# Second blocks: products of the gated unit end with the sixth attention head, gelus and mixing stand sooner, branch additions on GpSimd

## The chip, the cores and the metric

The kernel runs on one core of a Trainium2 chip. The metric is the device time of one execution in microseconds (us), the median of several runs. Engines are called TensorE (PE in the profile), VectorE (DVE), ScalarE (ACT), GpSimd (POOL) and SyncE (SP).

## What is computed

The reference is a small network over 256 tokens of 1024 features: two first blocks (differential attention with a dense gated layer, and a gated linear recurrence with a mixture of eight experts), a norm, and then two "second blocks" of one form. Only the second blocks are touched. Each of them has two halves that read the same normed input:

- a sparse attention with eight heads of 64 in two groups. For every head and each of two chunks of 128 queries there are three branches: a compressed one (32 compressed keys, computed for all heads at once) and two with full scores (masked differently). The three results are weighted by gates (a sigmoid of a projection, 24 columns) and added up:

```
o = gate[0] * o_compressed + gate[1] * o_first + gate[2] * o_second
```

- a gated unit: u and v are projections of 512 columns each; both go through a gelu, v through a layer norm, and then v is mixed over the tokens by a masked 128x128 matrix per group, gets a bias and is multiplied by u:

```
mlp = (mix(layer_norm(gelu(v))) + b) * gelu(u)
```

Each half is normed by its mean square, the two are put side by side (1024 features), multiplied by an output matrix and added to the residual. A gated feed-forward layer follows.

## The kernel before

The function `second` holds one second block. Matrix products of the projections are split into three (hi x hi, hi x lo, lo x hi; L264 to L266), so each weight is split on ScalarE (the hi part, L229) and VectorE (the lo part, L230), and each activation likewise (xh L286, xl L287, after a transpose `tr` L293 of 128x128 tiles).

The heads are taken in sixteen steps: chunk 0 with heads 0 to 3 and 4 to 7, then chunk 1 with the same; I call them the first to the sixteenth head. For each of them there are:

- `score` (L1652 to L1666): products into `sw` (L1657), for each of two branches a mask with row maximum on VectorE (p, L1664) and an exponential with a sum on ScalarE (p, L1665). Chunk 0 has 128 keys a branch, chunk 1 has 256.
- `turn` (L1668 to L1678): transposes into `pt` (L1672), then the copy pT to SBUF, by VectorE for chunk 0 (L1677) and ScalarE for chunk 1 (L1675).
- `value` (L1680 to L1687): products into `po` (L1686), which four heads share.
- `combine` (L1689 to L1699), once for four heads: a small factor from sums and gates, the product `att` (L1696) and two additions of 128x256 into `at` (L1699), one for each branch.

Around the heads four generators are advanced a piece at a time. `gated` (L1553 to L1581) makes the twelve pieces of the products `tw` for three groups of columns (348, 350 and 350 wide); after the second group it puts the two `ln` (gelu of v, statistics, layer norm) on a list called `small`, after the third the gates, two gelus of u, two `mix` (the products `mx` at L1599, then two VectorE operations into `mlp`, L1602 and L1604) and `half_norm` of the mlp. `half_norm` is: the sum of squares on ScalarE (junk, L326), a small t on VectorE (L319), a root r on GpSimd (L320), two scalings on ScalarE (L1540), then transposes and their hi and lo splits. `cmps` makes the compressed branch of both chunks: products `cs` (L1625), a softmax pc (L1629 to L1638), transposes `ct` (L1642), pcT (L1644), products `oc` (L1648) that start `at` (L1650). `ex` finishes what the compressed keys need.

What stands where is set by a table, PLAN: one string for each of the sixteen heads. After the scores of a head its letters are worked off: x is a step of `ex`, z of `gated`, c of `cmps`, s of the list `small`, t turns the oldest scored head if more than three are scored, v takes the value products of the oldest turned head, and o combines the oldest finished four. What is left over is done after the last head. Then comes `half_norm` of the attention half, and the output products `ac` (L258 to L260) run over the mlp half's features first. A scheduler then orders the instructions of each engine; every engine works its own list strictly in that order and waits for what an instruction reads, and for a free buffer.

Of the kernel before, what the change touches and what calls it, by code (L numbers as in the profile page):

```python
# [15 lines left out]
OP = mybir.AluOpType  # L16
# [5 lines left out]
FILL = (4, 0, 0, 0, 0, 1, 1, 1, 1)  # L22
N_AHEAD = (2, 0)
AHEAD = 3
PLAN = ["xzz", "xzz", "xzt", "xztv", "ztv", "ztv", "zsvst", "zcvst", "zcvst", "zcvst", "csvct", "csvst", "osvst", "ovst",
        "svst", "svst"]
TURN = ((0, 0), (1, 1))
N_KV = 2
N_P = 6
# [104 lines left out]
def body(ctx: ExitStack, tc: tile.TileContext, I, out, stop=None):  # L134
    nc = tc.nc
    V, A, T, GP = nc.vector, nc.scalar, nc.tensor, nc.gpsimd
# [18 lines left out]
    def G(s="g", dt=F32):  # L155
        return gp.tile([128, 512], dt, tag="g", name=nm(s))

    def G2(s="t", dt=F32):
        return tp.tile([128, 512], dt, tag="t", name=nm(s))
# [7 lines left out]
    def S(n, s="s"):  # L167
        return sp.tile([128, 16 if n <= 16 else 64], F32, tag="s" if n <= 16 else "sw", name=nm(s), bufs=N_S if n <= 16 else 1)[:, :n]
# [10 lines left out]
    def r3(ap, n):  # L179
        return ap.rearrange("p (a b) -> p a b", a=n)  # L180
# [1158 lines left out]
    def second(i, pj, fill, X):  # L1339
# [121 lines left out]
        for c, ps in enumerate(wide):  # L1461
            g = G("z1")
# [13 lines left out]
        for c, ps in enumerate(tok_wide(X, w, 0, 512, "zq")):  # L1476
            g = G2("zq")
# [3 lines left out]
            for kg in range(2):  # L1481
                t = G2("qhl", F32R)
# [9 lines left out]
        for c in range(2):  # L1492
            A.activation(seg2[:, c * 256:c * 256 + 256], ps[:, c * 256:c * 256 + 256], AF.Copy, scale=r[:, c:c + 1])
            srcs = [r3(seg1[c][:, 256:384], 2), r3(seg2[:, c * 256:c * 256 + 128], 2)]
            t = [G2("kd", F32R) for _ in range(2)]
# [9 lines left out]
        for hp in range(4):  # L1505
# [6 lines left out]
            g = G("qT", F32R)  # L1512
# [37 lines left out]
        for hf in range(2):  # L1550
            t = G("wsT")
# [100 lines left out]
        def score(c, h, sums):  # L1652
            g = h // 4
            nk = 128 * (c + 1)
            ps = PA("sw")
            for s in range(2):
                T.matmul(r3(ps[:, :2 * nk], 2), lhsT=q_ap(h, c), rhs=r3(kT[g][s], 2)[:, :, :nk], start=s == 0, stop=s == 1)  # L1657
            mx = S(2)
            p = GP2("p")
            tri = names["tri"][:, 128 - c * 128:256]  # L1660
            for br in range(2):
                sl = p[:, br * nk:br * nk + nk]
                o = br * 4 + h % 4
                V.tensor_tensor_reduce(sl, ps[:, br * nk:br * nk + nk], tri, -1.0, 3.0e38, OP.add, OP.min, mx[:, br:br + 1])  # L1664
                A.activation(sl, sl, AF.Exp, scale=-1.0, bias=mx[:, br:br + 1], accum_out=sums[:, o:o + 1])  # L1665
            return p  # L1666
# [22 lines left out]
        def combine(c, g, sums, po):  # L1689
            fac = S(8, "fac")  # L1690
            V.tensor_scalar(fac, sums, 1e-30, None, op0=OP.max)
            V.reciprocal(fac, fac)
            gv = gts[c].rearrange("p (h b) -> p b h", b=3)[:, 1:3, g * 4:g * 4 + 4]
            V.tensor_tensor(r3(fac, 2), r3(fac, 2), gv, op=OP.mult)
            t = G2("att")
            V.tensor_tensor(r3(t, 8), r3(po, 8), fac[:, :, None].to_broadcast([128, 8, 64]), op=OP.mult)  # L1696
            a = at[c][:, g * 256:g * 256 + 256]
            for br in range(2):
                V.tensor_tensor(a, a, t[:, br * 256:br * 256 + 256], op=OP.add)  # L1699

        def cmps():
            a, b = cmp_attn(1), cmp_attn(0)
# [37 lines left out]
        for c, g in ((0, 0), (0, 1), (1, 0), (1, 1)):  # L1740
            sums = S(8, "sums")
            po = PA("po")
            for h in range(g * 4, g * 4 + 4):
                scored.append((c, h, score(c, h, sums), sums, po))
                for what in PLAN[n]:
                    if what == "z":
                        step(zg)
                    elif what == "x":
                        steps(ex, 1)
                    elif what == "c":  # L1750
                        step(cm)
                    elif what == "s":
                        small_step()
                    elif what == "t" and len(scored) > AHEAD:
                        flush_t()
                    elif what == "v" and turned:
                        flush_v()
                    elif what == "o" and pend:
                        combine(*pend.pop(0))
                n += 1  # L1760
# [12 lines left out]
        while pend:  # L1773
            combine(*pend.pop(0))
# [118 lines left out]
```

## Time and profile before

| | us |
|---|---|
| median of three runs | 2278.92 |
| lowest and highest run | 2278.32, 2280.7 |
| the profiled execution | 2279.51 |
| its span | 2277.7 |

TensorE is busy 97% of the span, VectorE 80%, ScalarE 65%, GpSimd 3%. The mean granted clock of TensorE is 0.983 of full speed. Second block 0 takes about 1541 to 1905 us of the span and second block 1 about 1910 to 2277. A busy TensorE is not the same as a TensorE at its limit: busy time counts the matmuls' modelled spans at whatever clock was granted, so the granted clock has to be read beside it.

In the windows view one row is one stretch: from and to, its length, then for each engine its busy time with the number of instructions, then the granted clock, the DMA engines' share and GB/s. In the timeline a row is one instruction, or several of a kind in a row: its start, how long, engine, line, operation, what it writes and reads, its tile, how many, and in brackets the time the engine waited ahead of it and for whom. The records of an engine overlap a little, so what one instruction costs a full engine is the step from one start to the next.

### The profile page before, as it was taken

What the parts mean: (1) busy time and instruction counts of PE and PEld (TensorE: products, weight loads), DVE (VectorE), ACT (ScalarE), POOL (GpSimd) and SP (SyncE); (2) the same over time, 40 slices, a digit from 0 to 9 for tenths busy, and PEclk for the clock granted to TensorE, in tenths of its full rate; (3) what the DMA queues carried; (4) which work ended last, traced back from release to release, by engine and by line L of the source; (5) the groups of instructions that cost most, each with busy time, mean ns of one, the idle gap of its engine ahead of it and who ended that gap; (6) DMA issues with size and microseconds to landing.
All of it is one profiled execution on the core that took longest, in us unless ns stands there. A gap on an engine that the chain in (4) does not pass through costs nothing.

```text
span 2277.7 us, 36685 instructions
## 1 busy us (share of the span) xinstructions
PE 2208.9 (97%) x14081; PEld 1990.1 (87%) x14081; DVE 1828.3 (80%) x2734; ACT 1475.6 (65%) x2144; POOL 57.9 (3%) x72
## 2 busy tenths in 40 slices
PE   8999999998999999999999999999999999989998
PEld 7999999887878888888888888878899998989998
DVE  7765686767888888999898989889777779868776
ACT  6554467436777777776777767777665566766555
POOL 0000001000000000000000000000000001000000
PEclk9999999998999999999999999999999999989999
DMA  9445556126999999999999999987245554525550
GB/s 312 159 149 180 173 184 211 57 98 217 362 343 329 338 365 373 337 356 348 373 351 341 352 371 353 372 301 229 83 141 175 190 180 139 189 79 185 185 173 27
DMA packets 297111, 551.20 MB, mean 242 GB/s; under 512 B 10336, under 2 KB 132064, under 8 KB 296928
## 3 DMA queue, kind: packets, MB, share of 16 engines
q1 hardware_dynamic: 296928, 548.78, 68.6%
q8 instruction: 112, 1.84, 0.3%
q14 instruction: 71, 0.58, 0.1%
HBM read 547.70 MB, written 1.05 MB: 241 GB/s over the span
## 4 chain that ended last, share of the span: by engine, by line
PE 68%; DVE 5%; ACT 2%; issue 2%; POOL 1%; DMA 0%; POOLq 0%; DVEq 0%; SPq 0%; ACTq 0%
PE y L1208 5%; PE pg L266 4%; PE y L1207 4%; PE y L1206 4%; PE pg L264 4%; PE pg L265 4%; PE pu L266 4%; PE pu L264 4%; PE pu L265 4%; PE gu L258 4%; PE gu L260 4%; PE gu L259 4%; PE ac L258 2%; PE ac L259 2%; PE ac L260 2%
## 5 line engine op out<-in xcount | busy, mean ns | idle before, releaser
L230 DVE TENSOR_TENSOR loe<-ste,hie 128x1024 fp32r<-128x1024 f32 x448 | 520.3, 1221 | 12.4 <-ACT hie L229 4.2
L229 ACT ACTIVATE hie<-ste 128x1024 fp32r<-128x1024 f32 x448 | 439.5, 1053 | 23.7 <-PE ac L260 9.6
L230 DVE TENSOR_TENSOR lod<-std,hid 128x1024 fp32r<-128x1024 f32 x224 | 265.0, 1220 | 17.1 <-ACT hid L229 15.6
L229 ACT ACTIVATE hid<-std 128x1024 fp32r<-128x1024 f32 x224 | 221.5, 1057 | 4.9 <-PE pg L265 2.3
L266 PE MATMUL pu<-loe,eh 128*128 128x512 f32 x448 | 176.7, 394 | 1.4 <-DVE loe L230 1.4
L1207 PE MATMUL y<-hid,hl 128*128 128x512 f32 x448 | 175.8, 392 | 2.0 <-DVE hl L284 2.0
L264 PE MATMUL pg<-hie,eh 128*128 128x512 f32 x448 | 175.6, 392 | 0.3 <-ACT eh L286 0.3
L266 PE MATMUL pg<-loe,eh 128*128 128x512 f32 x448 | 175.6, 392 | 0.0
L265 PE MATMUL pg<-hie,el 128*128 128x512 f32 x448 | 174.7, 390 | 0.0
L264 PE MATMUL pu<-hie,eh 128*128 128x512 f32 x448 | 174.6, 390 | 0.0
L265 PE MATMUL pu<-hie,el 128*128 128x512 f32 x448 | 174.6, 390 | 0.0
L1206 PE MATMUL y<-hid,hh 128*128 128x512 f32 x448 | 173.4, 392 | 0.7 <-ACT hh L283 0.7
L1185 ACT ACTIVATE eh<-pg,cw 128x512 f32<-128x512 f32 x56 | 38.6, 689 | 203.6 <-PE pg L266 203.6
L1208 PE MATMUL y<-lod,hh 128*128 128x512 f32 x448 | 163.5, 407 | 0.8
L258 PE MATMUL gu<-xh,hig 128*128 128x256 f32 x528 | 150.6, 285 | 3.6 <-ACT xh L286 3.6
L230 DVE TENSOR_TENSOR lou<-stu,hiu 128x1024 fp32r<-128x1024 f32 x66 | 80.5, 1221 | 89.0 <-PE gu L259 73.8
L260 PE MATMUL gu<-xl,hig 128*128 128x256 f32 x528 | 150.0, 285 | 0.5 <-DVE xl L287 0.5
L259 PE MATMUL gu<-xh,lou 128*128 128x256 f32 x528 | 150.2, 284 | 0.0
L258 PE MATMUL gu<-xh,hiu 128*128 128x256 f32 x528 | 150.1, 284 | 0.0
L259 PE MATMUL gu<-xh,log 128*128 128x256 f32 x528 | 150.0, 284 | 0.0
L260 PE MATMUL gu<-xl,hiu 128*128 128x256 f32 x528 | 149.9, 284 | 0.0
L258 PE MATMUL ac<-hh,hidn 128*128 128x256 f32 x528 | 149.4, 283 | 0.0
(522 smaller groups left out, 6211.9 us busy)
## 6 DMA issues: line engine op xcount, KB each, us to landing
ste<-in_moe_w_gate_up_dram SPq DMA_DIRECT2D x224, 1024.0 KB, 7.3
std<-in_moe_w_down_dram SPq DMA_DIRECT2D x112, 1024.0 KB, 5.7
stg<-in_w_up_dram SPq DMA_DIRECT2D x22, 1024.0 KB, 5.1
stu<-in_w_up_dram SPq DMA_DIRECT2D x22, 1024.0 KB, 5.1
stdn<-in_w_down_dram SPq DMA_DIRECT2D x22, 1024.0 KB, 4.8
stg<-in_dense_w_gate_up_dram SPq DMA_DIRECT2D x11, 1024.0 KB, 5.0
stu<-in_dense_w_gate_up_dram SPq DMA_DIRECT2D x11, 1024.0 KB, 5.0
stdn<-in_dense_w_down_dram SPq DMA_DIRECT2D x11, 1024.0 KB, 5.0
```

The source lines that it names most:

```text
L229: A.activation(hi[:, :m], sq, AF.Copy)
L230: V.tensor_tensor(lo[:, :m], sq, hi.bitcast(F32)[:, :m], op=OP.subtract)
L258: T.matmul(o, lhsT=lh, rhs=rh, start=start, stop=False, **kw)
L259: T.matmul(o, lhsT=ll, rhs=rh, start=False, stop=False, **kw)
L260: T.matmul(o, lhsT=lh, rhs=rl, start=False, stop=stop, **kw)
L264: T.matmul(o, lhsT=xh, rhs=wh, start=start, stop=False, **kw)
L265: T.matmul(o, lhsT=xl, rhs=wh, start=False, stop=False, **kw)
L266: T.matmul(o, lhsT=xh, rhs=wl, start=False, stop=stop, **kw)
L1185: A.activation(t, pg, AF.Silu, scale=rc)
L1206: T.matmul(y[hf], lhsT=h[:, fs], rhs=a, start=opens, stop=False)
L1207: T.matmul(y[hf], lhsT=l[:, fs], rhs=a, start=False, stop=False)
L1208: T.matmul(y[hf], lhsT=h[:, fs], rhs=b, start=False, stop=ends)
```

## The change

The table PLAN is written anew, and six of the eight additions of a second block (all but those of the last four heads) are issued on GpSimd instead of VectorE.

```diff
--- before.py
+++ after.py
@@ -22,8 +22,8 @@
 FILL = (4, 0, 0, 0, 0, 1, 1, 1, 1)
 N_AHEAD = (2, 0)
 AHEAD = 3
-PLAN = ["xzz", "xzz", "xzt", "xztv", "ztv", "ztv", "zsvst", "zcvst", "zcvst", "zcvst", "csvct", "csvst", "osvst", "ovst",
-        "svst", "svst"]
+PLAN = ["xzz", "xzzz", "xzzt", "xzztv", "zztv", "zsvst", "csvst", "csvst", "csvst", "csvst", "csvct", "ovst", "svst", "svst",
+        "svst", "ovst"]
 TURN = ((0, 0), (1, 1))
 N_KV = 2
 N_P = 6
@@ -1695,8 +1695,9 @@
             t = G2("att")
             V.tensor_tensor(r3(t, 8), r3(po, 8), fac[:, :, None].to_broadcast([128, 8, 64]), op=OP.mult)
             a = at[c][:, g * 256:g * 256 + 256]
+            eng = V if (c, g) == (1, 1) else GP
             for br in range(2):
-                V.tensor_tensor(a, a, t[:, br * 256:br * 256 + 256], op=OP.add)
+                eng.tensor_tensor(a, a, t[:, br * 256:br * 256 + 256], op=OP.add)
 
         def cmps():
             a, b = cmp_attn(1), cmp_attn(0)
```

In the old table the twelfth z stands with the tenth head and combines with the thirteenth and fourteenth. In the new one the first six heads have 2, 3, 2, 2, 2 and 1 of them, list steps start with the sixth head, and o stands with the twelfth and the last head; the rest of the combines come after the loop. The arithmetic is the same. The two second blocks are changed alike.

On TensorE, where the gated products end. The names are: tw the gated products, pt the transposes, sw the scores, cs, ct and oc the compressed branch, mx the mixing, po the values. Before, in second block 0:

```order
L266 MATMUL tw_29153<-lozg_29269,xh_28318 128x350
L1642 MATMUL ct_29348<-keep,pc_29225 128x128 x2
L1672 MATMUL pt_29360<-keep,p_29147 128x128 x2
L1657 MATMUL sw_29365<-kT_28826,qT_28805 128x512
L1657 MATMUL sw_29365<-kT_28833,qT_28805 128x512
L1599 MATMUL mx_29508<-v_28853,wsT_28859 128x64
L1686 MATMUL po_29072<-z_7677_28420,pT_29319 128x64
L1686 MATMUL po_29072<-z_7735_28690,pT_29319 128x64
L1657 MATMUL sw_29392<-kT_28826,qT_28805 128x512
```

And now:

```order
L266 MATMUL tw_29103<-lozg_29163,xh_28318 128x350
L1672 MATMUL pt_29218<-keep,p_29019 128x128 x2
L1657 MATMUL sw_29223<-kT_28840,qT_28819 128x256
L1657 MATMUL sw_29223<-kT_28847,qT_28819 128x256
L1625 MATMUL cs_29232<-keepr,qT_28798 128x32 x4
L1625 MATMUL cs_29232<-keepr,qT_28805 128x32 x4
L1625 MATMUL cs_29232<-keepr,qT_28812 128x32 x4
L1625 MATMUL cs_29232<-keepr,qT_28819 128x32 x4
...
L1642 MATMUL ct_29338<-keep,pc_29249 128x128 x2
L1672 MATMUL pt_29355<-keep,p_29189 128x128 x2
L1599 MATMUL mx_29456<-v_28853,wsT_28859 128x64 x4
L1599 MATMUL mx_29456<-v_28853,wsT_28862 128x64 x4
```

Both compressed score groups (cs) and two of the first chunk's scores stood ahead of the last tw; now they stand behind it, and the mixing products follow twelve groups later, where all sixteen of chunk 0's mx come in one piece.

On VectorE, at the scores of the last three heads (p with 128x256), before. L1604 is the second operation of the mixing, L319 the t of the mlp half norm:

```order
L1604 TENSOR_TENSOR mlp_29517<-mlp_29517,u_28851 128x512
L1322 SCALAR_TENSOR_TENSOR u_28852<-gs_29482,u_28852 128x512
L1664 ISA p_29531,s_29530<-sw_29527,k_5801 128x256
L1664 ISA s_29530 128x1
L1664 ISA p_29531,s_29530<-sw_29527,k_5801 128x256
L1664 ISA s_29530 128x1
L1602 TENSOR_TENSOR mlp_29545<-mx_29536,keep 128x512
L1604 TENSOR_TENSOR mlp_29545<-mlp_29545,u_28852 128x512
L319 TENSOR_SCALAR t_29558<-s_29552 128x2
```

And now, with xl the lo split of the transposed mlp half:

```order
L1604 TENSOR_TENSOR mlp_29465<-mlp_29465,u_28851 128x512
L1604 TENSOR_TENSOR mlp_29481<-mlp_29481,u_28852 128x512
L1664 ISA p_29495,s_29494<-sw_29491,k_5801 128x256
...
L319 TENSOR_SCALAR t_29506<-s_29500 128x2
L1664 ISA p_29526,s_29525<-sw_29522,k_5801 128x256
...
L287 SCALAR_TENSOR_TENSOR xl_29537<-tr_29531,keep,xh_29536 128x256
L287 SCALAR_TENSOR_TENSOR xl_29552<-tr_29546,keep,xh_29551 128x256
L287 SCALAR_TENSOR_TENSOR xl_29537<-tr_29531,keep,xh_29536 128x256
L1664 ISA p_29568,s_29567<-sw_29564,k_5801 128x256
...
L287 SCALAR_TENSOR_TENSOR xl_29552<-tr_29546,keep,xh_29551 128x256
L1664 ISA p_29568,s_29567<-sw_29564,k_5801 128x256
```

The mixing's operations stood around the sixteenth head's scores; now they stand ahead of the fourteenth's, and t and the lo splits of the mlp half stand between the scores of the last two heads.

On ScalarE, at the same place, now (junk L326 is the sum of squares, L1540 the scaling, xh the hi split):

```order
L326 ACTIVATE junk_29501,s_29500<-mlp_29465 128x512
L1665 ACTIVATE p_29495,sums_29445<-p_29495,s_29494 128x256 x2
L326 ACTIVATE junk_29503,s_29500<-mlp_29481 128x512
L1675 ACTIVATE pT_29520<-pt_29515 128x512
L1540 ACTIVATE mlp_29465<-mlp_29465,r_29505 128x512
L1540 ACTIVATE mlp_29481<-mlp_29481,r_29505 128x512
L1665 ACTIVATE p_29526,sums_29445<-p_29526,s_29525 128x256 x2
L286 ACTIVATE xh_29536<-tr_29531,keep 128x256
L286 ACTIVATE xh_29551<-tr_29546,keep 128x256
L286 ACTIVATE xh_29536<-tr_29531,keep 128x256
L1675 ACTIVATE pT_29562<-pt_29557 128x512
L286 ACTIVATE xh_29551<-tr_29546,keep 128x256
```

Before, the hi splits stood behind the exponentials (L1665) of the last head; now three of them stand ahead of these, with pT copies (L1675) between.

## Rows read from the trace of the kernel before

**Rows 1.** The head of the page: the profiled span.

```profile
span 2277.7 us, 36685 instructions
```

**Rows 2.** Windows by stage, layer 0 and layer 1: length, then each engine's busy us.

```profile
1582.70:1614.40 31.70, 31.45 (x220) 29.89 (x220) 25.92 (x84) 20.30 (x59) 0.92 (x1) 1.00 0.63 206
1614.40:1635.20 20.80, 17.64 (x134) 15.75 (x132) 19.69 (x70) 16.32 (x49) 0.85 (x1) 1.00 0.14 51
1635.20:1645.90 10.70, 9.31 (x46) 9.31 (x47) 5.03 (x17) 7.20 (x18) 0.70 (x1) 0.53 0.01 2
...
1980.90:2002.00 21.10, 17.85 (x134) 15.82 (x132) 19.34 (x69) 15.61 (x46) 0.90 (x1) 0.96 0.15 51
```

**Rows 3.** Timeline of TensorE, layer 0: start us, length, line, tile, waits.

```profile
1614.29 0.32 PE L266 MATMUL tw<-lozg,xh 128*128 128x350 f32 x1
...
1632.43 0.61 PE L1672 MATMUL pt<-keep,p 128*128 128x128 f32 x4
1636.59 4.53 PE L1686 MATMUL po<-z,pT 128*128 128x64 f32 x20 [3.55 <-ACT pT L1675]
...
1644.54 1.38 PE L1686 MATMUL po<-z,pT 128*128 128x64 f32 x8
...
1651.60 0.44 PE L293 MATMUL tr<-keep,at 128*128 128x128 f32 x2 [0.60 <-ACT at L1540]
```

**Rows 4.** Short windows on TensorE: length, busy, granted clock, DMA, GB/s.

```profile
1635.00:1636.00 1.00, 0.00 (x0) 0.55 0.00 0
1645.00:1646.00 1.00, 1.00 (x9) 0.83 0.00 0
1911.00:1914.00 3.00, 1.96 (x11) 1.00 0.19 26
...
2045.00:2046.00 1.00, 1.00 (x6) 0.50 0.00 0
```

**Rows 5.** Timeline of TensorE, a shorter gap elsewhere.

```profile
2043.42 0.39 PE L258 MATMUL gu<-xh,hig 128*128 128x256 f32 x1 [1.79 <-ACT xh L286]
```

**Rows 6.** Timeline of TensorE, what groups of small products take.

```profile
1604.86 1.86 PE L1625 MATMUL cs<-keepr,qT 128*128 128x32 f32 x16
...
1625.46 1.04 PE L1672 MATMUL pt<-keep,p 128*128 128x128 f32 x8
1626.33 1.00 PE L1686 MATMUL po<-z,pT 128*128 128x64 f32 x8
...
1628.66 0.70 PE L1657 MATMUL sw<-kT,qT 128*128 128x512 f32 x2
1629.20 1.89 PE L1599 MATMUL mx<-v,wsT 128*128 128x64 f32 x16
```

**Rows 7.** Groups by line and shape, VectorE, 1582.7 to 1647.9: busy, mean ns.

```profile
L230 DVE TENSOR_TENSOR lowo<-stwo,hiwo 128x1024 fp32r<-128x1024 f32 x6 | 7.3, 1221 | 1.6 <-PE tw L266 0.9 <-issue 0.7
L1664 DVE CUSTOM_DVE_ANT_0 p<-sw,k 128x256 f32<-128x256 f32 x16 | 6.3, 416 | 0.1
...
L1664 DVE CUSTOM_DVE_ANT_0 p<-sw,k 128x128 f32<-128x128 f32 x16 | 4.1, 285 | 1.1 <-PE sw L1657 1.0
```

**Rows 8.** Timeline of VectorE, two 512-wide operations and the last head's mask.

```profile
1633.30 0.68 DVE L1604 TENSOR_TENSOR mlp<-mlp,u 128x512 f32<-128x512 f32 x1
1633.90 0.69 DVE L1322 SCALAR_TENSOR_TENSOR u<-gs,u 128x512 f32<-128x512 f32 x1
...
1634.84 0.42 DVE L1664 CUSTOM_DVE_ANT_0 p<-sw,k 128x256 f32<-128x256 f32 x1
```

**Rows 9.** Groups by line and shape, ScalarE, 1582.7 to 1647.9.

```profile
L1675 ACT ACTIVATE pT<-pt 128x512 f32<-128x512 f32 x8 | 4.6, 585 | 2.1 <-PE pt L1672 2.1
...
L286 ACT ACTIVATE xh<-tr,keep 128x256 fp32r<-128x256 f32 x4 | 1.8, 472 | 2.9 <-PE tr L293 2.7 <-DVE xl L287 0.2
```

**Rows 10.** Timeline of ScalarE, the scalings of the mlp half.

```profile
1638.64 1.34 ACT L1540 ACTIVATE mlp<-mlp,r 128x512 f32<-128x512 f32 x2 [0.53 <-POOL r L320]
```

**Rows 11.** One line's instructions: GpSimd's multiplies, ns min/median/max.

```profile
L366 POOL TENSOR_TENSOR sq<-sq,sq x11: 1282/1347/2751, 11.2 to 2248.3; 128x512 f32<-128x512 f32 x11
```

## The prediction

> **What bounds the kernel now.** I read the windows by stage first, because the change touches only the two second blocks, and in them only the stretch in which attention heads, gated unit and mixing share the engines. The profiled run took 2279.51 us, 0.6 above the median of 2278.92, with a span of 2277.7 [rows 1]: 1.8 us lie around it. In layer 0 the stretch falls into three parts [rows 2]. Until the last product of the gated unit at 1614.29 [rows 3] TensorE has no gap (31.45 of 31.70 us busy), and VectorE idles 5.8 of them. From there to 1635.20 it is the reverse: VectorE is busy 19.69 of 20.80 us, TensorE 17.64, so VectorE sets the pace. The third part is the end of the heads. The timeline of TensorE shows its start [rows 3]: a transpose issued at 1632.43, then nothing until 1636.59, after 3.55 us of waiting for ScalarE's copy pT of the last heads, whose scores VectorE had only just delivered. The granted clock fell to half (1.2 GHz) in that gap and was on its way back to full in 1645 to 1646 (0.83) [rows 4]. In 1635.2 to 1645.9 TensorE was busy 9.31 us at a mean clock of 0.53, so about half of it, 4.4 us, is what the low clock cost. The last value product ends at 1645.92 (1644.54 and 1.38) and the first transpose of the finished attention half starts at 1651.60 [rows 3]. Layer 1 repeats this some 366 us later, the middle part with nearly the same busy times [rows 2]. So two things could be won in each layer: the idle VectorE time ahead of the gated unit's end, and the 4.4 us of clock.
>
> **Part one: products end with the sixth head.** The twelve product groups are the same; what stood among them and now stands behind goes later. By the order on TensorE these are score products of four heads (two of the first chunk at 0.24, two of the second at 0.47), transposes of three first-chunk heads (0.22 each), value products of two such heads (0.39 each) and both compressed score groups, cs. Prices come from the rows of TensorE [rows 6]: eight transposes for two heads of the second chunk step 0.87, eight value products 0.84, two score products 0.54, sixteen cs records last 1.86 and step 1.70; first-chunk heads issue half as many, or half as wide. Sum: 0.48 + 0.94 + 0.66 + 0.78 + 3.40 = 6.3 us. The gated unit's end, which I call G, moves from 1614.4 to about 1608.2. Nothing else pays for that directly: TensorE had no gap there.
>
> But the end is not set by G alone. VectorE from the gates to the scores of the 14th head has, counted in its new order: one lo split (1.15), 6 pT copies (2.04), 4 first-chunk score branches (0.84), 12 second-chunk ones (4.08), 8 other 256-wide operations (2.72), 19 of 512 columns (11.4) and some 17 small ones (1.5), 23.7 us. A record overlaps the next by about 0.08 (0.68 long, 0.60 from start to start [rows 8]), so I took 0.60 for 512 columns, and 1.15, 0.34 and 0.21 for the means 1.221, 0.416 and 0.285 [rows 7]; the pT copies have the 256 columns of the 0.34. Two waits come on top. The mask of the second cs stands in VectorE's order ahead of the second v's gelu product and the layer norm of the first v; that cs ends on TensorE only at G + 4.7, and VectorE is there at about G + 3.2: 1.5 us. Some 0.5 more go to the exponentials of pc. The 14th head's scores are then ready at G + 26.0 to 26.6, 1634.5. Before, the **16th** head's were ready at 1635.2 [rows 8]. So although G comes 6 us sooner, VectorE is no further: its idle time ahead of G stays (it had 45.6 us of work through that head and has 44.9 now), because fewer heads' scores stand before G, not more.
>
> **Part two: gelus and mixing sooner.** The first mixing group, mx, now stands twelve groups behind the last product and reads the normed v. TensorE is there at G + 6.5 (cs twice, four transposes, three heads' scores, two value groups, one ct). The normed v ends on VectorE at about G + 9.8: the waits above, then mask, sum, two gelu products, statistics and two norm steps, 5 us from the second cs. So TensorE idles some 3.3 us there, 1614.7 to 1618, where it was busy before. As work this costs little, since VectorE sets the pace behind it. As a gap it matters: with gaps of 3.55 and 1.79 us [rows 3, 5] the granted clock went to half (0.55 and 0.50 in the windows), while in the three us with a gap of 1.04 (1.96 busy) it stayed full [rows 4].
>
> At the other end, mixing done sooner brings the half norm of the mlp, its scaling, four hi and four lo casts and its transposes ahead of the last heads on ScalarE, VectorE and TensorE. From the 14th head's scores: exponentials 0.6, squares 0.7, t 0.2, r on GpSimd 0.9, two scalings 1.3 [rows 10], 1.0 for the next head's exponentials, hi casts of 0.40 each and pT of 0.55 each [rows 9] between them. The value product of the 11th head waits for a pT behind the squares (TensorE idle about 2.5 us), the next for one behind three hi casts (1.6 us more), and from there, about 1641.4, TensorE has 6.2 us of transposes and value products of the last five heads. The last one ends at G + 39.4 = 1647.5, against 1645.9 before, **without** any clock loss: +1.6 us. Bounds: -0.3 if the casts slip between two waits, +2.6 if each cast waits for its transpose in turn.
>
> **Part three: additions on GpSimd.** Six of eight additions leave VectorE in each layer: 6 x 0.34 = 2.0 us of it, two of them before the 14th head's scores (counted above). The trace has no such addition on GpSimd. The nearest rows are its 128x512 multiplies, 1.35 us at the median and 2.75 at the worst, twice the columns [rows 11]; half is 0.65 to 1.4 us an addition, 8 us at most, spread over 25 us in which GpSimd does nothing but r. They are hidden unless the last of them delays the squares of the attention half; at the worst +1.0 a layer. The value I take is 0. The first three pairs end before the fourth, which stays on VectorE. The Trainium skill (GPSIMD Engine Reference, section 3.1) puts a two-operand addition at 1.96 times VectorE's time; here 1.35 against 0.68 us [rows 8, 11] for the same shape gives the same ratio, and by its section 8 the two engines share their way to SBUF and contend when VectorE reads two operands. By that rule each GpSimd addition could also stretch VectorE's; the 2.75 us maximum agrees that something stretches GpSimd, no run here shows VectorE slowed, and the sum with it would be about 1 us a layer longer.
>
> **Behind the heads.** The chain from the last value product to the first transpose of the attention half was 5.7 us. It loses about 1 us, because the half norm's t no longer stands behind a lo split; but the transposes stand twelve down-products earlier, 1.4 us, so TensorE has that much less to do meanwhile. The two cancel.
>
> **The clock in the changed kernel.** Each layer has two gaps that the trace's own gaps put near the border: about 3.3 us ahead of mx, and 2.5 us ahead of the 11th head's value product. A fall in the first doubles mx 1.7 [rows 6], one value group, the scores and ct that pcT and the gelus wait for: +3.0 us on the chain. A fall in the second costs +2.4, both +5.4. Both estimates of gaps are a hand count over mixed queues, and TensorE's waits may spread over several instructions, so I take one fall per layer: 1.6 + 3.0 = +4.6 us a layer, +9.2 in all, and 2278.9 + 9.2 = **2288 us**.
>
> **Rivals.** (a) Both gaps lose the clock: +1.6 + 5.4 = +7.0 a layer, 2293 us. For it: both gaps are longer than 1.79 us. Against it: they are counted, not seen. (b) Neither does: +1.6 a layer, 2282 us, no difference that can be measured. For it: a TensorE that is fed in drops, as in 1614.4 to 1635.2 where it was busy 85% with a clock of 1.00 [rows 2]. (c) The change does what it says: VectorE's two waits are filled by other heads' scores, the chain of the mlp hides behind them, the last heads come without a gap and at full clock. The old gap's clock loss is gone (-4.4) and the shorter wait brings about -1.6 more: -6 a layer, 2267 us. It decides if the 14th head's scores are out before about G + 24 = 1632. Against it: 23.7 us of VectorE work without any wait already fill that. (d) GpSimd's additions stretch to the worst row and hold up the squares: +1.0 a layer on any of these, no case of its own.
>
> **How the numbers follow.** Chances: forecast 0.37, (a) 0.16, (b) 0.26, (c) 0.21. A measurement of this kernel can tell about 0.2%, 4.6 us. Cases forecast and (a) are slower by more; (b) lies inside, with a small part of the forecast that falls below 2283.5 if its first term comes out at -0.3 or the fall is short; (c) is faster. Faster 0.21, same 0.28, slower 0.51. The range leaves out the better half of (c) and the tail of (a): 2268 to 2294.
>
> **What would show it.** Right: the last gated product near 1608; TensorE idle about 3 us ahead of mx with the granted clock at 0.50 behind it; VectorE waiting for a cs product; pT of the 11th and 12th head late behind the squares and hi casts; the last value product at 1648 to 1651; additions of 0.65 to 1.4 us on GpSimd. Wrong: the 14th head's scores before 1632, or a granted clock of 1.00 from 1615 to 1645. Then (b) or (c) holds. If the additions slow VectorE's own operations beyond 0.42 and 0.68 us, part three is mis-sized.

## The result, and the profile after

The changed kernel took 2299.64 us (median of three runs, 2294.26 to 2300.28) against 2278.92: a ratio of 1.0083, 95% interval 1.0069 to 1.0096; 19 us slower by the ratio, 20.7 between the medians. The direction was forecast; 2288 us was too little, and the range ended at 2294. The profiled execution is the quickest of the three, 2294.26 us with a span of 2292.4 and a mean granted clock of 0.982; the other two have 0.980. As an estimate from these rounded clocks, 2292.4 x 0.018 x 2 = 83 us were spent at half clock against 2298 x 0.020 x 2 = 92 us; 9 us more at half clock cost up to 4.7 us of TensorE's work, which could be most of the spread of the three runs. Only the quickest one was profiled.

Where the time went is read from two marks in each second block, a group of small products of the block's key path (hT, L1403; the second of its two such groups) and the first product of the norm behind the attention (ms, L335). Timeline of TensorE, before: start us, length, line.

```profile
1582.15 0.63 PE L1403 MATMUL hT<-k,hr 62*128 62x30 f32 x4
...
1670.63 0.58 PE L335 MATMUL ms<-keep,sq 128*128 128x1 f32 x4
...
1947.37 0.63 PE L1403 MATMUL hT<-k,hr 62*128 62x30 f32 x4
...
2036.50 1.05 PE L335 MATMUL ms<-keep,sq 128*128 128x1 f32 x8
```

And after:

```profile
1579.40 0.63 PE L1403 MATMUL hT<-k,hr 62*128 62x30 f32 x4
...
1675.80 1.38 PE L335 MATMUL ms<-keep,sq 128*128 128x1 f32 x10
...
1953.83 0.63 PE L1403 MATMUL hT<-k,hr 62*128 62x30 f32 x4
...
2051.83 1.02 PE L335 MATMUL ms<-keep,sq 128*128 128x1 f32 x8
```

Block 0 went from 88.48 to 96.40 us between the marks, block 1 from 89.13 to 98.00: +7.9 and +8.9, 16.8 in all. (This execution was 2.75 us earlier at the first mark: from 1530 to 1541 us, ahead of the second blocks, its mean granted clock was 0.84 against 0.72 before.) The forecast had +4.6 for each.

**The first loss: the clock falls without a gap.** Windows of one microsecond on TensorE, after: length, busy share, granted clock.

```profile
1607.00:1608.00 1.00, 1.00 (x11) 1.00 0.82 315
1608.00:1609.00 1.00, 1.00 (x8) 0.58 1.00 414
...
1612.00:1613.00 1.00, 0.42 (x2) 0.50 0.00 0
...
1621.00:1622.00 1.00, 0.95 (x5) 0.60 0.00 0
1622.00:1623.00 1.00, 1.00 (x8) 1.00 0.00 0
```

The clock went to half at about 1608.2 (0.58 in that window), with TensorE fully busy, and stayed there for 13.6 us, to 1621.8. The wait ahead of the mixing came 4 us later. In block 1 it was the same: half clock from 1983.6 to 2000.7, and the wait ahead of the mixing only at 1988.3. The timeline of TensorE shows what it was doing:

```profile
1603.72 0.32 PE L266 MATMUL tw<-lozg,xh 128*128 128x350 f32 x1
...
1606.99 2.36 PE L1625 MATMUL cs<-keepr,qT 128*128 128x32 f32 x16
...
1614.91 3.65 PE L1599 MATMUL mx<-v,wsT 128*128 128x64 f32 x16 [2.49 <-ACT p L1665]
...
1620.60 0.63 PE L1642 MATMUL ct<-keep,pc 128*128 128x128 f32 x2
```

The last dense product starts at 1603.72. What follows are products of 32, 64 and 128 columns, and two groups of scores: the second cs group already takes 2.36 us instead of the 1.86 of [rows 6], the mixing 3.65 instead of 1.89. Before, the same cs products stood between dense ones, and the granted clock was 1.00 through that stretch [rows 2]. What hangs on it is read on ScalarE's timeline and on VectorE's. ScalarE:

```profile
1621.27 0.38 ACT L1644 ACTIVATE pcT<-ct 128x256 f32<-128x256 f32 x1 [4.59 <-PE ct L1642]
1621.55 0.62 ACT L1318 ACTIVATE gs<-u 128x512 f32<-128x512 f32 x1
```

VectorE over that stretch and up to the 14th head's second mask:

```profile
1609.39 0.42 DVE L1629 TENSOR_TENSOR pc<-cs,k 128x256 f32<-128x256 f32 x1 [2.09 <-PE cs L1625]
...
1618.79 0.17 DVE L1589 BATCH_NORM_AGGREGATE s<-s 128x2 f32<-128x6 f32 x1
1623.15 0.69 DVE L1319 SCALAR_TENSOR_TENSOR gt<-gs,u 128x512 f32<-128x512 f32 x1 [4.19 <-ACT p L1665]
...
1635.83 0.41 DVE L1664 CUSTOM_DVE_ANT_0 p<-sw,k 128x256 f32<-128x256 f32 x1
```

ScalarE stood 4.59 us at pcT, waiting for the transposes ct that a half-speed TensorE reached at 1620.60; behind pcT on ScalarE is the gelu of u (gs, 1621.55), and for that VectorE stood 4.19 us, until 1623.15. (The gelu itself ended at 1622.17; the line names the exponential that ended at 1623.15, and why VectorE stood this last microsecond is not shown. In block 1 the wait at the same place is 3.30 us and ends with the gelu.) From the gates to the scores of the 14th head, which end at 1636.2, VectorE needed 32.3 us and not 26.0 to 26.6.

**The second loss: the mlp's chain ahead of the last heads.** TensorE's timeline at the end of the heads:

```profile
1638.18 0.93 PE L1686 MATMUL po<-z,pT 128*128 128x64 f32 x6 [1.83 <-ACT pT L1675]
...
1643.19 1.10 PE L1686 MATMUL po<-z,pT 128*128 128x64 f32 x8 [0.69 <-ACT pT L1675]
...
1649.01 1.00 PE L1686 MATMUL po<-z,pT 128*128 128x64 f32 x8
...
1655.22 0.44 PE L293 MATMUL tr<-keep,at 128*128 128x128 f32 x2 [1.69 <-ACT at L1540]
```

Its clock there, in windows of one microsecond:

```profile
1637.00:1638.00 1.00, 0.00 (x0) 1.00 0.00 0
...
1639.00:1640.00 1.00, 0.66 (x4) 0.50 0.00 0
...
1642.00:1643.00 1.00, 0.51 (x3) 0.86 0.00 0
```

The waits for pT are 1.83 and 0.69 us, the clock falls behind the first of them, for 3.4 us (1638.9 to 1642.3), and the last value product ends at 1650.0.

**The third: a root on GpSimd.** The first transpose of the attention half stands behind a wait of 1.69 us, against 0.60 [rows 3]. On VectorE the half norm's t now comes first and the lo split of the next weight right behind it; on GpSimd the root r of that half norm takes 1.65 us, against 0.70 us for the same shape elsewhere. VectorE's timeline:

```profile
1652.51 0.17 DVE L319 TENSOR_SCALAR t<-s 128x2 f32<-128x2 f32 x1 [0.85 <-ACT junk L326]
1652.62 1.22 DVE L230 TENSOR_TENSOR lowo<-stwo,hiwo 128x1024 fp32r<-128x1024 f32 x1
```

GpSimd at the same time:

```profile
1652.76 1.65 POOL L320 TENSOR_TENSOR r<-t,keep 128x2 f32<-128x2 f32 x1 [4.05 <-DVE t L319]
```

### The profile page after: what moved, and what is told of

Its sections match the earlier page's. It is cut to its first block, busy times and chain, and to the rows that moved or that the text cites. A ratio compares the mean times of both kernels' runs of the same rounds, so it can differ in the third digit from the quotient of the medians.

```text
span 2292.4 us, 36676 instructions
## 1 busy us (share of the span) xinstructions
PE 2214.3 (97%) x14081; PEld 1991.3 (87%) x14081; DVE 1826.5 (80%) x2722; ACT 1477.5 (64%) x2144; POOL 68.4 (3%) x84
## 5 line engine op out<-in xcount | busy, mean ns | idle before, releaser
L230 DVE TENSOR_TENSOR lod<-std,hid 128x1024 fp32r<-128x1024 f32 x224 | 264.9, 1218 | 17.1 <-ACT hid L229 15.7
```

Of the source, the lines that this page charges most:

```text
L230: V.tensor_tensor(lo[:, :m], sq, hi.bitcast(F32)[:, :m], op=OP.subtract)
```

## The experiments

The experiments were timed in three batches, each beside the kernel before on the same chip; times in us below are between medians, and where a ratio gives another number, both stand. The last two columns are TensorE's mean granted clock in the two stretches of heads, 1600 to 1660 and 1965 to 2030 us of each profiled execution.

| kernel | median us | ratio to before, 95% interval | block 0 | block 1 |
|---|---|---|---|---|
| before | 2278 to 2280 | 1 | 0.91 | 0.92 |
| changed | 2299.64 | 1.0083 [1.0069, 1.0096] | 0.86 | 0.84 |
| e1_adds | 2277.26 | 0.9988 [0.9980, 0.9997] | 0.94 | 0.95 |
| e2_plan | 2298.85 | 1.0086 [1.0072, 1.0099] | 0.80 | 0.92 |
| e3_cs_early | 2281.42 | 1.0016 [1.0005, 1.0026] | 0.94 | 0.97 |
| e4_mlp_late | 2287.44 | 1.0036 [1.0023, 1.0048] | 0.83 | 0.95 |
| e5_both_late | 2269.62 | 0.9964 [0.9950, 0.9977] | 0.97 | 1.00 |
| e6_dense_fill | 2292.18 | 1.0057 [1.0043, 1.0071] | 0.89 | 0.89 |
| e7_gap_fill | 2273.21 | 0.9976 [0.9964, 0.9987] | 0.97 | 1.00 |
| e8_old_mlp_late | 2274.50 | 0.9972 [0.9962, 0.9982] | 1.00 | 0.92 |
| e9_best_adds_dve | 2273.73 | 0.9975 [0.9965, 0.9985] | 0.97 | 0.97 |
| e10_best_fill | 2270.59 | 0.9957 [0.9945, 0.9969] | 1.00 | 1.00 |

**The two halves of the change alone.** `e1_adds` has the old table and the additions on GpSimd, `e2_plan` the new table and all additions on VectorE.

> The old table, with only the six additions a layer moved to GpSimd. Theory (the table makes the loss): they are hidden at 0.73 us each, and VectorE gets back at most 2 us a layer, of which little is on the path: 2277 to 2280 us. Rival (the additions make it, by themselves or by holding up GpSimd's roots): at least 2284 us, with ScalarE's squares of the attention half waiting for GpSimd.

> The new table alone, all additions on VectorE. Theory (the table makes the loss): 2295 to 2301 us, the granted clock at half from the second group of compressed scores on as in the changed kernel. Rival (the additions make a part): 2290 us or less. The root on GpSimd of the attention half, 1.65 us in the changed kernel, tells which neighbour stretches it: if it still takes over 1.5 us here, it is VectorE's lo split and not the additions.

The additions alone are 1.8 us faster (2.7 by the ratio), the table alone makes the whole loss. Its clock is only in part that of the changed kernel: in block 0 half clock begins at the second cs group (at 1611.3), but in block 1 both cs groups run at the full clock and the fall comes in the wait ahead of the mixing, at 1993.6. The root tells the two sides apart as well. In `e2_plan` it takes 0.70 us, and there the lo split stands ahead of t, and no addition runs on GpSimd; VectorE's timeline there:

```profile
1658.55 1.22 DVE L230 TENSOR_TENSOR lowo<-stwo,hiwo 128x1024 fp32r<-128x1024 f32 x1 [0.96 <-PE ac L259]
1659.69 0.16 DVE L319 TENSOR_SCALAR t<-s 128x2 f32<-128x2 f32 x1
```

And GpSimd's:

```profile
1659.93 0.70 POOL L320 TENSOR_TENSOR r<-t,keep 128x2 f32<-128x2 f32 x1 [19.20 <-DVE t L319]
```

So my wording of that test was too narrow: what goes with the long root is a lo split that runs at the same time. In the changed kernel, in `e3_cs_early` and in `e6_dense_fill` the split starts 0.13 to 0.15 us ahead of the root, which then takes 1.64 to 1.66 us; in `e2_plan` (additions on VectorE) and in `e4_mlp_late` and `e5_both_late` (on GpSimd) it ends first, and the root takes 0.70 or 0.71. That neither the new table nor the additions are needed shows in the trace of the kernel before, which has four roots of this shape elsewhere (L342) behind a 128x1024 subtraction that starts 0.16 or 0.17 us ahead of them; they take 1.61 or 1.62 us, and without such a neighbour 0.69 to 0.71. One of the four, VectorE and then GpSimd, before:

```profile
1690.02 1.22 DVE L230 TENSOR_TENSOR lodn<-stdn,hidn 128x1024 fp32r<-128x1024 f32 x1
```

```profile
1690.18 1.62 POOL L342 TENSOR_TENSOR r<-s,keep 128x2 f32<-128x2 f32 x1 [8.89 <-DVE s L341]
```

**The compressed scores back among the dense products.** The changed kernel, its table with the two c moved:

```diff
-"xzztv", "zztv", "zsvst", "csvst", "csvst", "csvst", "csvst", "csvct"
+"xzztv", "czcztv", "zsvst", "svst", "svst", "csvst", "csvst", "csvct"
```

> The changed kernel, with both groups of compressed scores (cs, 32 columns a product) back among the dense gated products, three letters of the table earlier; everything behind them in the same order. Theory (the two groups behind the last dense product bring the clock to half and the chain ct, pcT, gelus then waits for a slow TensorE): the clock is full until a gap ahead of the mixing or stays full, VectorE's wait of 4.2 us at the gelu of u shrinks to under 1.5 us, 4 to 6 us a layer come back: 2287 to 2292 us. Rival (the chain of the mlp ahead of the last heads makes nearly all of the loss): 2296 us or more.

18 us come back (15 by the ratios), more than the theory's 8 to 12. Windows of TensorE, where the changed kernel had half clock from 1608.2 to 1621.8:

```profile
1612.00:1613.00 1.00, 0.49 (x5) 1.00 0.00 0
...
1615.00:1616.00 1.00, 1.00 (x9) 0.72 0.00 0
...
1618.00:1619.00 1.00, 1.00 (x4) 0.58 0.00 0
```

In this stretch the clock now falls only at 1615.4, behind a wait of 1.42 us ahead of the mixing, and is back at 1618.8; the fall at the end of the heads is still there. VectorE has no wait over 0.3 us from 1612 to 1622. But this edit does two things, since the masks of pc come out earlier on VectorE too. `e6_dense_fill` therefore leaves the order as it is and changes only what TensorE does there:

```diff
             for h in range(8):
                 for s in range(2):
                     T.matmul(ps[:, h * 32:h * 32 + 32], ...
+                for j in range(2):
+                    T.matmul(ps[:, 256:512], lhsT=q_ap(h, j), rhs=qT[h // 2][:, 0:256], start=True, stop=True)
```

> The changed kernel, in its order, with sixteen products of 256 columns added to each group of compressed scores (nobody reads their result; 32 x 0.12 = 3.8 us of TensorE work a layer at the full clock). Theory (what lowers the clock behind the last dense product is that TensorE has only small products there, not that it waits): the granted clock stays at 1.00 through the compressed scores, falls later if at all, and VectorE's wait of 4.2 us at the gelu of u shrinks below 2 us: 2284 to 2297 us in spite of the added work. Rival (the loss is the place of the compressed scores in the queue, and the clock only goes along): the chain gets 3.8 us longer a layer, 2303 us or more.

Its windows of one microsecond on TensorE:

```profile
1608.00:1609.00 1.00, 1.00 (x12) 1.00 0.41 45
...
1612.00:1613.00 1.00, 1.00 (x12) 1.00 0.00 0
...
1626.00:1627.00 1.00, 1.00 (x7) 0.88 0.00 0
...
1639.00:1640.00 1.00, 1.00 (x5) 0.50 0.00 0
```

With the wider products between them the cs groups run at the full clock (their last dense product starts at 1605.92), and so does everything up to 1626.8. VectorE's wait at the gelu is gone. The kernel is 7.5 us quicker than the changed one (6 by the ratios) although TensorE has 64 x 0.12 = 7.7 us more to do: the clock was worth at least that gain. Not all is won, because the clock then falls at 1626.8, for 13.7 us. What the filler does not tell apart is width and waiting: it also closes the wait ahead of the mixing (0.15 us instead of 2.49), since TensorE gets there later. And the later fall comes behind a wait of 1.32 us that ended at 1624.5. How the gain of `e3_cs_early` divides between the clock and VectorE's earlier masks is not settled beyond that bound.

**The half norm of the mlp held back.** In the changed kernel, `small_step` does not touch the half norm while heads are still being scored:

```diff
         def small_step():
             while small:
+                if len(small) == 1 and n < 16:
+                    return
```

> The changed kernel, with the half norm of the mlp (squares, root, scaling, transposes, splits) not begun before the last head's scores. Rival to the clock theory (this chain, standing ahead of the last heads on ScalarE, makes the loss): TensorE's waits of 1.8 and 0.7 us for pT there go, the last value product ends 4 us sooner, 2290 us or less. Clock theory: the fall behind the compressed scores stays, only the second gap changes, 0 to 2.5 us a layer: 2294 to 2300 us.

12 us come back (11 by the ratios): in the range of the rival, and more than the clock theory allowed. It is not even in the two blocks. Between the marks block 0 has 95.1 us (96.4 in the changed kernel) and block 1 90.9 (98.0). Not all of it is the half norm's place, because the first fall differs too, in a stretch that this edit leaves alone: both cs groups run at the full clock here (1.85 us). In the six stretches with this order of products (us; the wait of TensorE is the one just ahead of the fall):

| stretch | second cs group | clock falls at | wait of TensorE | half clock for | VectorE's wait at the gelu | between the marks, against before |
|---|---|---|---|---|---|---|
| changed, block 0 | 2.36 | 1608.2 | none | 13.6 | 4.19 | +7.9 |
| changed, block 1 | 2.56 | 1983.6 | none | 17.1 | 3.30 | +8.9 |
| `e2_plan`, block 0 | 2.04 | 1611.3 | none | 13.7 | 4.52 | +10.0 |
| `e2_plan`, block 1 | 1.85 | 1993.6 | 3.77 | 6.8 | 3.29 | +6.6 |
| `e4_mlp_late`, block 0 | 1.85 | 1613.3 | 0.40 | 10.2 | 4.16 | +6.6 |
| `e4_mlp_late`, block 1 | 1.85 | 1988.7 | 3.77 | 6.8 | 3.29 | +1.8 |

The clock fell without a wait in three of them and in or behind a wait in the other three; in all six the mixing ran at half clock and VectorE then stood 3.3 to 4.5 us at the gelu. Like first falls stand in the two blocks 1 of `e2_plan` and `e4_mlp_late`: 95.7 against 90.9 us, so the held-back half norm is worth nearer to 4.8 us in a block (the additions differ as well) than the whole 7 that block 1 gained.

In block 0 of `e4_mlp_late` the clock falls once more (windows of one microsecond):

```profile
1627.00:1628.00 1.00, 0.00 (x0) 1.00 0.00 0
...
1630.00:1631.00 1.00, 1.00 (x5) 0.66 0.00 0
...
1639.00:1640.00 1.00, 1.00 (x5) 0.50 0.00 0
```

TensorE is busy when it falls at 1630.3, but it had waited 1.81 us for a mask of VectorE until 1628.1. In block 1 that wait is 0.89 us, and no second fall follows. In block 0 of the changed kernel the wait is 1.81 us as well and no fall follows it there, so why it comes in the one block and not in the other is left open.

**Both at once.**

> The changed kernel with both edits of before at once: the compressed scores back among the dense products and the half norm of the mlp not ahead of the last head's scores. Each alone took most of the loss away (2281 and 2287 us, from 2299), so they do not add up. Theory (both act through the same granted clock: one fall leads to the late chain that makes the next gap): 2274 to 2280 us, no better than the kernel before by more than 5. Rival (two separate losses of 17 and 12 us, that add up): 2270 us.

My theory fell: the two gains add up (18.2 and 12.2 us from 2299.6 make 2269.2; by the ratios 15 and 11 where 27 are measured), and `e5_both_late` with 2269.62 us is quicker than both kernels. The clock stays at full through all of block 1 (windows over the two stretches of heads: length, busy us, clock):

```profile
1600.00:1660.00 60.00, 57.20 (x434) 0.97 0.26 87
1965.00:2030.00 65.00, 61.10 (x478) 1.00 0.26 86
```

So the loss was not in the aim of the table but in two of its places. This is near the time that rival (c) gave, 2267 us, though for another kernel than the one it spoke of; its condition holds here, with the 14th head's scores out at 1630.9, 21.4 us behind the last gated product, and the heads end at the full clock and with few waits.

**The clock at the end of the heads, in the old order.** On top of `e1_adds`:

```diff
+        dm = PB("dm")
+        for k in range(24):
+            T.matmul(dm[:, 0:256], lhsT=q_ap(k % 8, k // 8 % 2), rhs=qT[k % 4][:, 0:256], start=True, stop=True)
         while scored:
```

> The old table with the additions on GpSimd (2277 us), plus 24 products of 256 columns (2.9 us at the full clock, nobody reads them) where TensorE waits ahead of the last heads' value products. Theory (the half clock behind that gap costs some 4 us a layer): the clock stays at 1.00 until the value products end, and 2 to 4 us a layer come back: 2269 to 2274 us. Rival (the end of the heads is set by the copies on ScalarE, so TensorE's clock there costs nothing): 2276 to 2280 us.

The same two windows for this kernel:

```profile
1600.00:1660.00 60.00, 57.53 (x439) 0.97 0.24 81
1965.00:2030.00 65.00, 62.93 (x498) 1.00 0.32 102
```

By the medians this is 4 us quicker than `e1_adds`, from work that nobody reads, put where TensorE waited; by the ratios it is 2.7, and the two intervals touch (0.9964 to 0.9987 and 0.9980 to 0.9997), so the gain is likely and its size is not settled. In block 1 the clock never falls and the stretch between the marks takes 85.95 us (87.98 in `e1_adds`); in block 0 it falls for 3.4 us instead of 6.8, and the stretch takes 86.42 (86.52). The prediction's 4.4 us a block for the half clock of the kernel before was the busy time lost; of that some 2 us were on the path, by this one execution.

**What the rest tells of the best version.** `e8_old_mlp_late` is `e1_adds` with the held-back half norm; `e9_best_adds_dve` is `e5_both_late` with all additions on VectorE; `e10_best_fill` is `e5_both_late` with twelve products of 256 columns ahead of the first mixing group.

> The old table with the additions on GpSimd (2277 us), and only the half norm of the mlp held back until the last head's scores: the gated products end with the tenth head as before. It tells what the earlier end of the gated products gives in the version that beat both kernels (2269.6 us: compressed scores among the dense products, half norm held back). Theory (the earlier end lets the mixing be done before the last heads and takes away the gap ahead of their value products): without it the gap stays, 2274 to 2280 us. Rival (all of that gain is the half norm's place): 2267 to 2272 us.

> The version of 2269.6 us (compressed scores among the dense products, half norm held back) with all additions on VectorE. Theory (VectorE sets the pace in the second half of the heads, so 2 us of it a layer are worth something there): 2271 to 2274 us. Rival (the additions stand where VectorE waits anyway): 2268 to 2271 us.

> The version of 2269.6 us with twelve products of 256 columns, read by nobody, put ahead of the first mixing products, where TensorE waits 1.4 us in layer 0 and the clock then falls for some 4 us (in layer 1 it stays full). Theory (the fall follows from too few products there): no half clock in layer 0 between 1610 and 1625 us, the added 1.4 us a layer lie in the wait; 2266 to 2270 us. Rival (the added products delay the chain to the pcT and the gelus): 2271 to 2275 us.

The first two medians lie in their theories' ranges, the third between its two. But their intervals overlap with that of `e5_both_late` (0.9950 to 0.9977), so what the earlier end of the gated products, the additions and the filler are worth in that version is not told apart; the medians of the three lie 1 to 5 us above that of `e5_both_late`. `e10_best_fill` does what was expected of the clock, in the same two windows:

```profile
1600.00:1660.00 60.00, 57.79 (x450) 1.00 0.25 82
1965.00:2030.00 65.00, 62.19 (x489) 1.00 0.28 87
```

but no time can be measured from it, and what sets the end in that version is not shown. By the medians the additions and the held-back half norm in the old table (`e8_old_mlp_late`, 5.3 us faster than before) give a good half of what the mended new table gives (8.7).

## Why the prediction was right or wrong

The step that failed is the clock term: one fall a layer, begun by the gap ahead of the mixing, worth +3.0 us. There were two falls a layer, the first began without a gap, and the path through that stretch came out 6 us late. A second term was wrong behind the heads. For block 0 the parts are: the gated unit's end 1.6 us better than forecast, from there to the last value product 3.7 us worse, behind the heads 1.1 us worse; with +4.6 that makes the +7.9 but for 0.1.

**The gated unit's end: right.** 1603.72 against 1614.29, and 2.75 of that was there at the block's first mark: 7.8 us, forecast 6.2. (By its own row a second-chunk head's two score products step 0.54 us, where the sum has 0.47; that is 0.14 us in all.)

**VectorE is no further for it: right.** The wait for the second cs is 2.09 us (forecast 1.5), and the 14th head's scores end at 1636.2 where before the 16th's did at 1635.2 [rows 8]. But they end 6 us later than G + 26.3. VectorE's work on the way took 24.9 us (counted: 23.7) and its waits 7.5 (counted: 2.0), 4.2 of them at the gelu.

**The gap ahead of the mixing: right in place and size** (2.49 us in block 0, 3.6 in block 1; forecast 3.3), **wrong as the cause of the fall.** The step that failed is "As a gap it matters": I compared only gaps, since the falls in my rows followed gaps [rows 3 to 5]. In the changed kernel the clock had fallen 4 us before the gap, with a busy share of 1.00, in a run of products of 32 to 128 columns and scores. With wider products among them in `e6_dense_fill` it did not fall there. In block 1 of `e2_plan` and of `e4_mlp_late`, though, the fall did come in the gap, as forecast, and the block of `e2_plan`, with both falls, lost 6.6 us, near the +7.0 of rival (a). So the mechanism behind the term was there in all stretches: a half-speed mixing, value group, scores and ct held up pcT and the gelu, by 3.3 us in each block 1 and 4.2 to 4.5 in each block 0, where the term has +3.0. Mis-sized was the whole of the stretch, 6 us late and not 3; the rest was VectorE's other waits and its longer work.

**One fall a layer: wrong, it was two.** Rival (a), both falls and 2293 us, was the nearest; its "they are counted, not seen" was no argument for the milder case. The second gap was 1.83 and 0.69 us (forecast 2.5 and 1.6) and its fall lasted 3.4 us.

**The end of the heads: mis-sized through the first step.** The last value product ended at G + 46.1, not G + 39.4; 6 of these 6.7 us are the 14th head's lateness. The chain that I put behind it (pT behind the squares and the hi casts) is there as described. What it is worth, +1.6 and +2.4 a layer together in the forecast, is not far from the 4.8 us between the two blocks 1 with like first falls.

**Behind the heads: wrong.** I let a gain of 1 us (t no longer behind a lo split) cancel 1.4 us of lost cover. The gain was taken back on GpSimd, whose root ran beside that same split and took 0.95 us longer; TensorE's wait grew by 1.1 us a block. The trace before already had such long roots (L342, 1.62 us); the forecast left them out.

**The additions: right in their own length, wrong on VectorE.** They take 0.73 us each, inside 0.65 to 1.4 (in `e1_adds` 0.72 to 1.11), and `e1_adds` is not held up by them: ScalarE's squares of the attention half wait 2.1 us in two blocks, before 3.4. All of the line's instructions in the changed kernel (ns, min/median/max):

```profile
L1700 POOL TENSOR_TENSOR at<-at,att x12: 724/727/737, 1632.9 to 2024.0; 128x256 f32<-128x256 f32 x12
L1700 DVE TENSOR_TENSOR at<-at,att x4: 426/426/427, 1650.8 to 2027.3; 128x256 f32<-128x256 f32 x4
```

The kernel with them alone is 1.8 us faster, and VectorE's own additions keep their length (0.426 us, before 0.422). But the sign that I had named, a VectorE operation beyond 0.68 us, did come. The second operation of the mixing, before and in the changed kernel:

```profile
L1604 DVE TENSOR_TENSOR mlp<-mlp,u x4: 684/688/692, 1633.3 to 2002.5; 128x512 f32<-128x512 f32 x4
```

```profile
L1604 DVE TENSOR_TENSOR mlp<-mlp,u x4: 678/892/1110, 1633.8 to 2010.9; 128x512 f32<-128x512 f32 x4
```

The first one in each block starts while an addition runs on GpSimd and takes 1.1 us. In `e1_adds` and `e5_both_late` it is up to 1.22 and 1.12, and in `e2_plan` and `e9_best_adds_dve`, with all additions on VectorE, at most 0.69. So by an estimate a block gets back some 1.6 of the 2.0 us that part three took off VectorE. The Trainium skill's rule (GPSIMD Engine Reference, section 8) on the shared way to SBUF, contention with VectorE instructions that have two SBUF inputs, agrees with both: an addition stretched VectorE's multiply, for which the forecast took nothing, and VectorE's two-operand split stretched GpSimd's small root from 0.70 to 1.65 us, which it did not have.

## What to carry to other kernels

When dense products are pulled forward, look at what is left behind them: a stretch of narrow products (32 to 128 columns) lost the full clock in three of six cases here while TensorE was busy, in the others behind a wait, and a chain that passes through it twice paid for it each time. Keep such products spread among the wide ones, and put a chain of another branch that shares ScalarE behind the last scores, not ahead of them; undone in these two places, the same table went from 19 us slower to 8 or 9 us faster. And when an instruction's order on VectorE changes by one place, or work moves to GpSimd, read what the other of the two does at that moment.

## What the runs showed of the hardware

- The granted clock fell with TensorE at a busy share of 1.00 and no wait behind the last dense product: at 1608.2 and 1983.6 in the changed kernel and at 1611.3 in `e2_plan`, in runs of products of 32, 64 and 128 columns and scores. The same run kept the full clock until a wait (0.40 to 3.77 us) in block 1 of `e2_plan` and in both blocks of `e4_mlp_late`. With products of 256 columns put among the same small ones (`e6_dense_fill`) the clock stayed at 1.00 from 1606 to 1626.
- A root of 128x2 on GpSimd took 0.69 to 0.71 us, and 1.61 to 1.66 us when a 128x1024 subtraction of VectorE (1.22 us) began 0.13 to 0.17 us before it: in both blocks of three kernels, and four times in the kernel before at another line. The subtraction kept its 1.22 us.
- A 128x512 multiply of two operands on VectorE took 0.68 to 0.69 us, and 1.1 to 1.2 us when it began while GpSimd ran an addition (changed kernel, `e1_adds`, `e5_both_late`).
- Executions of one kernel differed by up to 9 us, and the mean granted clock with them: `e3_cs_early` took 2279.5 us at 0.987 and 2288.4 at 0.981.
